# Hybrid encoder layer in fp32: second weight operand ahead only where the first pass runs, the shift sums moved ahead, transposes in two sets of banks, partial sums multiplied where they are added

## The chip, the cores and the metric

The kernel runs on one core of a Trainium2 chip. The metric is the device time of one execution in microseconds (us). TensorE (PE) does the matmuls, VectorE (DVE) and ScalarE (ACT) the elementwise work, GpSimd (POOL) clears a few tiles and issues some transfers, SyncE (SP) issues nearly all transfers (DMAs). Each engine takes its own instructions strictly in the order in which they stand.

## The reference, cut to what matters

```python
mod = silu(c) @ w_ada + b_ada                 # c: one row of 2048
shift, scale, gate = split(mod, 3)
h = rmsnorm(x, pre_g) * (1 + scale) + shift   # x: 1024 rows of 2048
proj = h @ w_in                               # 2048 x 4608
q, k, v, gate_a, u, gate_p = split(proj)
y_a = windowed_gqa(q, k, v, ...) * silu(gate_a)
y_p = multiscale_pool(u, ...) * silu(gate_p)
g_a, g_p = split(sigmoid(h @ w_merge + b_merge))   # 2048 x 4096
merged = g_a * (y_a @ w_br_attn) + g_p * (y_p @ w_br_pool)
out = x + gate * rmsnorm(merged @ w_out, post_g)
```

All of it is in fp32.

## The kernel before

**Matmuls.** Each fp32 operand is split into a high and a low part (`split`: ACT writes `hi`, DVE writes `lo`), and a product is three matmuls (high by high, high by low, low by high). `h @ w_in` and `h @ w_merge` are made with Strassen's seven products (Winograd's form) for two blocks of 128 output columns, a "pair". `strassen` is a generator that makes one pair, a product per step: X from B11, V from T3, Z from T2, X from B21, V from T4, Z from T1, Z from B22 (X, V, Z are banks of PSUM; B11 ... B22 are operands made from `h`; each weight operand is `whi`/`wlo`, made from a loaded `raw` or from a difference `ws`). Each bank is read by ACT or DVE before its next product may start. A product with four row blocks is 12 matmuls of 128x512; in the ramp it has two row blocks and six matmuls.

**Stages.** (1) The start, to about 90 us: `x` is transposed (`XT` banks on PE, taken to `xT` by ACT and DVE), matrix-vector sums (`GEMV`) give the scale and later the shift of the first columns (`PM` turns a sum into columns), and the first four pairs are multiplied without their shift by plain blocks (`PB`); each finished block `c` is copied by ACT and stored to `ramp_d` by POOL's queue (`put_by`). (2) The ramp, to about 212 us: pairs 4 to 7 for the first four row blocks (`js` 0 and 1), then all eight for the rest (`js` 2 and 3). In the second half each stored part is loaded, multiplied by `rb` (`times`, L285) and added to a product (L260). (3) The first pass, to about 723 us: the other pairs, for the first half of the rows of the weights. (4) From about 723 us the second pass adds the other half to the parts in `part_d`; its start also builds four sums of `w_out` (`sw` loaded, summed on DVE, stored to `ws_dS`), and from about 860 us it carries attention. (5) The branches and the output product.

**What sets the order.** The start is an order written by hand: instructions passed through `keep` keep the program's order on their engine. Elsewhere a scheduler orders each engine's instructions from its own costs, so a generator that yields at another place can stand otherwise on DVE, ACT and SP far from the edit. `late` holds a pair back, so that its last product (Z from B22) is made two steps into the next pair. `SEEDED` names two PSUM tags of one bank each; the tags `mm`, `at`, `sc` have two banks.

Of the kernel before, what the change touches and what calls it, by code (L numbers as in the profile page):

```python
# [43 lines left out]
def encoder_layer(ctx: ExitStack, tc: tile.TileContext, x, c, table, w_ada, b_ada, pre_g,  # L44
# [167 lines left out]
    def strassen(w, n0, rows, js, op, ev, finish, part=None, raws=None, given=(), bias=None, factor=None):  # L212
# [70 lines left out]
        def times(*blks):  # L283
            for blk in blks if bias else ():
                nc.vector.tensor_tensor(parts[blk], parts[blk], factor[:, int(blk[1]) - 1], ALU.mult)  # L285
# [4 lines left out]
        first, second = next(wts), next(wts)  # L290
        product(first, "B11", bx, True)
        nc.scalar.activation(bz, bx, AF.Copy)
# [23 lines left out]
        product(prep(a12), "B22", bz)  # L316
        result("12", bz)
# [120 lines left out]
    def norm_row(si):  # L438
        square_of(si, 2, False)
        square_of(si, 3, True)  # L440
        square_of(si, 1, si % 2 == 0, xts[si, 2 + (si % 2 == 0)])
# [218 lines left out]
    def raw_operands(j, s, turned=False):  # L660

        for kh, name in enumerate(("B11", "B21") if s == 0 else ("B12", "B22")):
# [3 lines left out]
            keep(nc.scalar.activation(hi, src, AF.Copy, scale=a))  # L666
            keep(nc.vector.scalar_tensor_tensor(lo, src, a, f32(hi), op0=ALU.mult, op1=ALU.subtract))
# [60 lines left out]
    def ramp_gen(js, i, parts, last, **kw):  # L728
        w, n0 = weight_of(RAMP_ORDER[i])
        dst = block(part_d, RAMP_ORDER[i]) if last else block(ramp_d[i], 0)  # L730
        return strassen(w, n0, rows_in_turn(0), js, op, ev, to_dram(dst), parts, raws.pop(0), **kw)
# [6 lines left out]
    def fetch_wide(half, j):  # L738

        wide[half, j] = wp.tile([P, 2, 512], F32, tag="raw", name=uid("wide"), bufs=4)  # L740
        n0 = COL_K + half * 512
        keep(load(wide[half, j], w_in[2 * j * P:(2 * j + 2) * P, n0:n0 + 512].rearrange("(k p) n -> p k n", p=P)))
# [8 lines left out]
    fetch_wide(0, 0)  # L751
    for si in range(4, 8):
        fetch_row(si, (0,))
    claim_turned(range(4))
# [85 lines left out]
    def turn_next():  # L840
        s, ks = rounds.popleft()
        turn_part(s, ks, SEEDED)
        for k in ks:
            take_turned(s, k, False)
# [22 lines left out]
    for k in range(2):  # L867
        take_turned(0, k, k == 1)
# [1061 lines left out]
```

## Time and profile before

| | us |
|---|---|
| median of 3 runs | 2108.41 (2107.81 to 2109.29) |
| the profiled execution, its own time | 2110.96 |
| its span (first to last instruction) | 2109.2 |
| PE busy | 2076.3 |
| DVE busy | 1552.8 |
| ACT busy | 1113.3 |
| POOL busy | 47.3 |
| mean granted TensorE clock | 0.997 |

The time is that of one core from end to end; 1.8 us of the profiled execution's time lie outside its span. Busy times of the engines overlap. In rows of the timeline, the first number is the start in us, the second the duration, and the bracket says how long the engine stood idle before it and what ended that. Rows with "x4" join four instructions.

### The profile page before, as it was taken

To read this page: it belongs to the slowest core of one execution; us is meant where nothing else is said; L and a number is where in the kernel's file an instruction comes from. 1 tells how busy PE (TensorE), PEld (TensorE's weight loads), DVE (VectorE), ACT (ScalarE), POOL (GpSimd) and SP (SyncE) were. 2 spreads that over 40 slices of the span, in tenths; PEclk is the share of its full clock that TensorE was granted. 3 is DMA by queue.
4 is the path that set the end of the run, shared out by engine and by line. 5 is a ranking of instruction groups with operands and counts; after the bars stand their busy time and mean duration, and the time that the engine had idled before them with its cause. 6 is when DMAs were issued, how large, how long until landed. Compare 5 with 4: busy or idle time off the path is not lost.

```text
span 2109.2 us, 29056 instructions
## 1 busy us (share of the span) xinstructions
PE 2076.3 (98%) x9526; PEld 1703.7 (81%) x9526; DVE 1552.8 (74%) x2799; ACT 1113.3 (53%) x2126; POOL 47.3 (2%) x150
## 2 busy tenths in 40 slices
PE   8999999999999999999999999999999999999998
PEld 5677888788888887788888888888888788888886
DVE  4689677777566775777777678857957977889667
ACT  5664444444564633665666544333745644767654
POOL 1100000001000000000000000010000000000000
PEclk9999999999999999999999999999999999999999
DMA  9877777887575467654545476765745566686897
GB/s 357 305 255 253 262 262 223 281 289 246 186 242 191 136 224 239 232 166 161 194 160 162 153 243 223 223 236 174 254 153 170 176 199 194 221 313 203 298 332 246
DMA packets 302608, 476.61 MB, mean 226 GB/s; under 512 B 24306, under 2 KB 139098, under 8 KB 302456
## 3 DMA queue, kind: packets, MB, share of 16 engines
q1 hardware_dynamic: 296192, 457.79, 66.1%
q0 software_dynamic: 5200, 14.85, 1.8%
q10 hardware_dynamic: 1064, 2.11, 0.3%
q8 instruction: 75, 1.23, 0.3%
q14 instruction: 77, 0.63, 0.1%
HBM read 346.70 MB, written 130.05 MB: 226 GB/s over the span
## 4 chain that ended last, share of the span: by engine, by line
PE 86%; DVE 5%; DMA 5%; issue 2%; ACT 1%; POOL 0%; SPq 0%; DVEq 0%; POOLq 0%; ACTq 0%
PE Z L237 28%; PE X L237 19%; PE V L237 18%; PE Z L1637 2%; PE Z L1638 2%; PE Z L1639 2%; PE V L1638 1%; PE V L1637 1%; PE V L1639 1%; PE X L1639 1%; PE X L1638 1%; PE X L1637 1%; DVE wlo L97 1%; PE PT L1347 1%; DMA bias_d<-line_d 1%
## 5 line engine op out<-in xcount | busy, mean ns | idle before, releaser
L96 ACT ACTIVATE whi<-raw 128x512 fp32r<-128x512 f32 (+1 forms) x528 | 314.7, 600 | 487.6 <-PE Z L237 238.0
L97 DVE TENSOR_TENSOR wlo<-raw,whi 128x512 fp32r<-128x512 f32 (+1 forms) x528 | 339.4, 649 | 149.8 <-PE Z L237 112.9
L97 DVE TENSOR_TENSOR wlo<-wr,whi 128x512 fp32r<-128x512 f32 x224 | 150.6, 689 | 51.3 <-ACT whi L96 47.3
L96 ACT ACTIVATE whi<-wr 128x512 fp32r<-128x512 f32 x224 | 138.5, 629 | 86.2 <-DVE wlo L97 31.7
L103 DVE TENSOR_TENSOR raw<-raw,raw 128x512 f32<-128x512 f32 x76 | 52.4, 690 | 98.7 <-DMA raw<-in_w_merge_dram 60.8
L96 ACT ACTIVATE whi<-ws 128x512 fp32r<-128x512 f32 (+1 forms) x88 | 53.0, 603 | 77.1 <-PE X L237 62.2
L237 PE MATMUL X<-B11h,whi 128*128 128x512 f32 x328 | 90.5, 394 | 2.4 <-DVE part L103 2.4
L237 PE MATMUL Z<-T2h,whi 128*128 128x512 f32 x328 | 89.2, 391 | 3.2 <-ACT whi L96 3.0
L237 PE MATMUL Z<-T2h,wlo 128*128 128x512 f32 x328 | 89.5, 392 | 2.2 <-DVE wlo L97 2.2
L237 PE MATMUL Z<-T1l,whi 128*128 128x512 f32 x328 | 89.4, 390 | 1.1 <-DVE T1l L97 1.1
L237 PE MATMUL V<-T3h,whi 128*128 128x512 f32 x328 | 89.5, 392 | 0.8 <-DVE u L103 0.8
L237 PE MATMUL X<-B11l,whi 128*128 128x512 f32 x328 | 90.1, 393 | 0.0
L237 PE MATMUL X<-B21h,whi 128*128 128x512 f32 x328 | 90.0, 393 | 0.0
L237 PE MATMUL Z<-B22h,whi 128*128 128x512 f32 x328 | 89.9, 392 | 0.0
L237 PE MATMUL Z<-T1h,whi 128*128 128x512 f32 x328 | 89.7, 390 | 0.0
L237 PE MATMUL V<-T4h,whi 128*128 128x512 f32 x328 | 89.5, 391 | 0.0
L237 PE MATMUL X<-B21l,whi 128*128 128x512 f32 x328 | 89.3, 391 | 0.0
L237 PE MATMUL X<-B21h,wlo 128*128 128x512 f32 x328 | 89.1, 391 | 0.0
L237 PE MATMUL X<-B11h,wlo 128*128 128x512 f32 x328 | 88.9, 390 | 0.0
L237 PE MATMUL Z<-B22l,whi 128*128 128x512 f32 x328 | 88.9, 390 | 0.0
L237 PE MATMUL V<-T3l,whi 128*128 128x512 f32 x328 | 88.9, 390 | 0.0
L237 PE MATMUL V<-T4h,wlo 128*128 128x512 f32 x328 | 88.9, 390 | 0.0
(419 smaller groups left out, 4913.0 us busy)
## 6 DMA issues: line engine op xcount, KB each, us to landing
part<-part_d SPq DMA_DIRECT2D x136, 256.0 KB, 4.7
ada<-in_w_ada_dram SPq DMA_DIRECT2D x128, 256.0 KB, 5.7
raw<-in_w_merge_dram SPq DMA_DIRECT2D x64, 512.0 KB, 5.0
wr<-ws_dS SPq DMA_DIRECT2D x60, 512.0 KB, 5.3
raw<-in_w_in_dram SPq DMA_DIRECT2D x56, 512.0 KB, 4.4
wr<-in_w_out_dram SPq DMA_DIRECT2D x48, 512.0 KB, 5.1
proj_d<-part SPq DMA_DIRECT2D x68, 256.0 KB, 2.2
sw<-in_w_out_dram SPq DMA_DIRECT2D x64, 256.0 KB, 5.2
```

The source lines that it names most:

```text
L96: ins = (nc.scalar.activation(hi, src, AF.Copy), nc.vector.tensor_tensor(lo, src, f32(hi), ALU.subtract))
L97: nc.vector.tensor_tensor(lo, src, f32(hi), ALU.subtract))
L103: return (eng or nc.vector).tensor_tensor(o, a, b, ALU.add)
L237: nc.tensor.matmul(ps, w_[:, i], op[mov][j][m_], start=fresh and i == 0 and n == 0, stop=i == nj - 1 and n == 2, skip_group_check=True)
L1347: nc.tensor.transpose(pt[:, i * P:(i + 1) * P], p[:, i * P:(i + 1) * P], ident)
L1637: nc.tensor.matmul(pb, hi, w[0], start=first, stop=False, skip_group_check=True)
L1638: nc.tensor.matmul(pb, lo, w[0], start=False, stop=False, skip_group_check=True)
L1639: nc.tensor.matmul(pb, hi, w[1], start=False, stop=last, skip_group_check=True)
```

## The change

In words:

- `strassen` has a new argument `ahead`. With it (ramp and first pass) the second weight operand (`ws`) is still made before the first product; without it (all later pairs of `strassen`) it is made after the first step.
- `times` takes one part and is called just before or after the product to which the part is added: "22" after the V product is issued, "21" after Z from T2, "11" after X from B21, "12" after Z from B22. Before, the multiplications stood one to three steps earlier.
- At the start, `fetch_wide` loads the first wide weights in two halves; the sum for the scale columns (`g[4]`) is taken ahead of the first transposes; `xT` is taken from the `XT` banks right after the raw operands; two squares move from ACT to DVE.
- The shift `GEMV` and its scaled rows (`scale_row`) stand ahead of block (2,"22"), its `PM` right behind that block. The four rounds of transposes of tiles 4 to 7 use `SEEDED` and `at` banks in turn, and the takes stand behind the shifted operands (`put_shifted`) they were ahead of; the third weight operand (`first_given(2)`) moves up.
- The pool of evictions in the ramp's second half has 7 buffers instead of 6; the raw weights of the second pair of the first pass are loaded at step 0 instead of 2.

```diff
-        def times(*blks):
-            for blk in blks if bias else ():
+        def times(blk):
+            if bias:
                 nc.vector.tensor_tensor(parts[blk], parts[blk], factor[:, int(blk[1]) - 1], ALU.mult)
...
-        first, second = next(wts), next(wts)
+        first = next(wts)
+        second = next(wts) if ahead else None
         product(first, "B11", bx, True)
         nc.scalar.activation(bz, bx, AF.Copy)
+        yield
+        product(second or next(wts), "T3", bv, True)
         times("22")
-        yield
-        product(second, "T3", bv, True)
         p7 = read("p7", "22", bv)
-        times("21")
         yield
         product(next(wts), "T2", bz)
+        times("21")
         u2 = read("u2", "21", bz)
-        times("11", "12")
         yield
         product(prep(a12), "B21", bx)
+        times("11")
         result("11", bx)
...
         product(prep(a12), "B22", bz)
+        times("12")
         result("12", bz)
...
-    fetch_wide(0, 0)
+    fetch_wide(0, 0, 0, 256)
     for si in range(4, 8):
         fetch_row(si, (0,))
+    fetch_wide(0, 0, 256, 512)
...
+    g[4]()
     turn_part(0, (0, 1), SEEDED)
-    g[4]()
     turn_part(0, (2, 3), ("mm", "mm"))
-    wide_weights(0, 0)()
-    raw_operands(0, 0, True)
-    for k in (2, 3):
-        take_turned(0, k, k == 3)
+    raw_operands(0, 0, True, lambda: wide_weights(0, 0)())
+    for k in (0, 2, 1, 3):
+        take_turned(0, k, k % 2 == 1)
...
     raw_operands(0, 1, True)
-    for k in range(2):
-        take_turned(0, k, k == 1)
     turn_part(1, (2, 3), SEEDED)
...
     put_by(3, "21")
-    turn_next()
-    sums_over()
-    whole_block(2, "22")
-    put_by(2, "22")
     for si in range(4, 8):
         scale_row(si)
     g = row_sums(scz, shift_tile, shift_columns)
     for step in g[:4]:
         step()
+    sums_over()
+    whole_block(2, "22")
+    put_by(2, "22")
+    g[4]()
     first_given(0)
     first_given(1)
-    turn_next()
-    g[4]()
-    whole_block(3, "12")
+    takes = turn_next(SEEDED)
     put_shifted("B11", lambda j: block_of(j, 0, 0), shift(0))
-    put_by(3, "12")
-    turn_next()
+    for take in takes:
+        take()
...
     put_shifted("T3", lambda j: block_of(j, 0, 1), lambda j: dif[:, j:j + 1])
+    whole_block(3, "12")
+    put_by(3, "12")
+    takes = turn_next(("at", "at"))
+    for take in takes:
+        take()
+    put_shifted("T2", t2.__getitem__, shift(1))
     whole_block(3, "22")
     put_by(3, "22")
-    turn_next()
-    put_shifted("T2", t2.__getitem__, shift(1))
+    first_given(2)
+    takes = turn_next(SEEDED) + turn_next(("at", "at"))
     put_shifted("B21", lambda j: block_of(j, 1, 0), shift(1))
-    first_given(2)
+    for take in takes:
+        take()
     fill_last()
...
-    pev = ramp.enter_context(pool("rampev", 6))
+    pev = ramp.enter_context(pool("rampev", 7))
```

The matmuls of the products stay in their order outside the first 340 or so of PE's rows, but for one exchange of two neighbouring groups. What moves on the other engines shows at four places.

ACT, the first block of the start, before. `whi<-wide` is the high part of the first weights, B11h ... B22h the first operands, `XT_461`, `XT_478` and so on the banks that hold transposed `x`:

```order
L515 ACTIVATE acc_456<-GEMV_439 128x256
L787 ACTIVATE whi_488<-wide_166 128x512
L666 ACTIVATE B11h_190<-XT_461,modc 128x512
L666 ACTIVATE B21h_194<-XT_462,modc 128x512
L482 ACTIVATE xT_184<-XT_478 128x512
L666 ACTIVATE B12h_202<-XT_512,modc 128x512
L666 ACTIVATE B22h_198<-XT_513,modc 128x512
L482 ACTIVATE xT_176<-XT_461 128x512
```

The same place after:

```order
L518 ACTIVATE acc_457<-GEMV_440 128x256
L669 ACTIVATE B11h_191<-XT_469,modc 128x512
L795 ACTIVATE whi_490<-wide_166 128x512
L669 ACTIVATE B21h_195<-XT_470,modc 128x512
L485 ACTIVATE xT_177<-XT_469 128x512
L485 ACTIVATE xT_185<-XT_479 128x512
L669 ACTIVATE B12h_203<-XT_515,modc 128x512
L669 ACTIVATE B22h_199<-XT_516,modc 128x512
```

The copy that empties the first `SEEDED` bank (`xT<-XT_461`, now `XT_469`) moved ahead of the operands of the second half of the rows; on DVE the copy of the other `SEEDED` bank moved likewise.

ACT ahead of the third product of the ramp's first pair, before. `Z<-X` copies the first product's bank, which the third product (Z from T2) adds to:

```order
L810 ACTIVATE c_1015<-PB_1002 128x512
L482 ACTIVATE xT_350<-XT_1018 128x512
L482 ACTIVATE xT_1_353<-XT_1019 128x512
L712 ACTIVATE T2h_358<-tf_850,modc 128x512
L712 ACTIVATE T2h_366<-tf_852,modc 128x512
L712 ACTIVATE B21h_194<-xT_180,modc 128x512
L712 ACTIVATE B21h_210<-xT_0_188,modc 128x512
L292 ACTIVATE Z_1054<-X_1053 128x512
L251 ACTIVATE p_240_1069<-V_1055 128x512
L96 ACTIVATE whi_1040<-raw_370 128x256
```

After:

```order
L818 ACTIVATE c_1008<-PB_995 128x512
L96 ACTIVATE whi_1013<-raw_371 128x256
L717 ACTIVATE B21h_195<-xT_181,modc 128x512
L717 ACTIVATE B21h_211<-xT_0_189,modc 128x512
L485 ACTIVATE xT_343<-XT_1017 128x512
L485 ACTIVATE xT_347<-XT_1018 128x512
L485 ACTIVATE xT_351<-XT_1027 128x512
L485 ACTIVATE xT_1_354<-XT_1028 128x512
L717 ACTIVATE B22h_199<-xT_183,modc 128x512
L717 ACTIVATE B22h_215<-xT_1_190,modc 128x512
L293 ACTIVATE Z_1055<-X_1054 128x512
```

The third weights (`whi<-raw`) moved ahead of the copy Z<-X, and so did two more takes of `xT` and both B22h.

DVE in the ramp's second half, at the pair whose parts are numbered 2091 to 2097, before. `part<-part,rb` is `times`, `wlo<-raw` the low part of the third product's weights:

```order
L285 TENSOR_TENSOR part_2095<-part_2095,rb 128x512
L285 TENSOR_TENSOR part_2097<-part_2097,rb 128x512
L260 SCALAR_TENSOR_TENSOR p_519_2165<-V_2140,bias_1775,part_2091 128x512
L97 TENSOR_TENSOR wlo_2183<-raw_1831,whi_2182 128x256
L97 TENSOR_TENSOR wlo_2206<-raw_1831,whi_2205 128x256
```

After (the parts are numbered 2090 to 2096):

```order
L285 TENSOR_TENSOR part_2094<-part_2094,rb 128x512
L106 TENSOR_TENSOR ws_2251<-raw_1953 128x256
L97 TENSOR_TENSOR wlo_2183<-raw_1832,whi_2182 128x256
L260 SCALAR_TENSOR_TENSOR p_519_2165<-V_2140,bias_1776,part_2090 128x512
L97 TENSOR_TENSOR wlo_2205<-raw_1832,whi_2204 128x256
L97 TENSOR_TENSOR wlo_2219<-raw_1832,whi_2218 128x256
```

The multiplication of the fourth part (2097, now 2096) is no longer ahead of that `wlo`; it stands 14 rows further on.

DVE near the start of the second pass, before. `raw<-raw,raw` is the first sum of the next pair's weights and reads both its `raw` tiles; `part<-X` empties the X bank that the next pair's first product fills:

```order
L97 TENSOR_TENSOR wlo_7757<-raw_7609,whi_7756 128x512
L97 TENSOR_TENSOR wlo_7793<-raw_7777,whi_7792 128x512
L103 TENSOR_TENSOR u_1584_7714<-u_1584_7714,part_7615 128x512
L103 TENSOR_TENSOR raw_7777<-raw_7777,raw_7779 128x4x128
L106 TENSOR_TENSOR raw_7777<-raw_7777 128x4x128
L103 TENSOR_TENSOR part_7617<-X_7621,part_7617 128x512
```

After:

```order
L97 TENSOR_TENSOR wlo_7758<-raw_7610,whi_7757 128x512
L103 TENSOR_TENSOR raw_7778<-raw_7778,raw_7780 128x4x128
L97 TENSOR_TENSOR wlo_7794<-raw_7778,whi_7793 128x512
L103 TENSOR_TENSOR u_1584_7715<-u_1584_7715,part_7616 128x512
L106 TENSOR_TENSOR sw_7691<-sw_7689,sw_7691 128x512
L106 TENSOR_TENSOR raw_7778<-raw_7778 128x4x128
L106 TENSOR_TENSOR sw_7693<-sw_7693,sw_7691 128x512
L103 TENSOR_TENSOR part_7618<-X_7622,part_7618 128x512
```

The sum that reads both `raw` tiles moved up two rows, and two sums of `w_out` (`sw`) came between it and `part<-X`. On SP, the load of the second of these `raw` tiles stands at the same place behind four loads of `sw`, but the store `ws_dS4` that the last of them waits for moved up five rows:

```order
L1083 DMA ws_dS_97<-sw_7520 128x512
L335 DMA proj_d<-u_1553_7546 128x512
L209 DMA part_7613<-part_d 128x512
L209 DMA part_7615<-part_d 128x512
L335 DMA proj_d<-p_1544_7496 128x512
L209 DMA part_7617<-part_d 128x512
L209 DMA part_7619<-part_d 128x512
L1083 DMA ws_dS_100<-sw_7526 128x512
L1072 DMA sw_7688<-in_w_out_dram 128x512
```

```order
L1092 DMA ws_dS_97<-sw_7521 128x512
L1092 DMA ws_dS_100<-sw_7527 128x512
L337 DMA proj_d<-part_7455 128x512
L1081 DMA sw_7689<-in_w_out_dram 128x512
L337 DMA proj_d<-u_1553_7547 128x512
L209 DMA part_7614<-part_d 128x512
L209 DMA part_7616<-part_d 128x512
L209 DMA part_7618<-part_d 128x512
```

The first of the two is before, the second after: `ws_dS_100` (the fourth store of a round) now stands right behind the third instead of behind six transfers.

More of the change, by code (lines that the diff above doesn't have):

```diff
@@ L210, in load_parts, with strassen @@
         return parts
-    def strassen(w, n0, rows, js, op, ev, finish, part=None, raws=None, given=(), bias=None, factor=None):
+    def strassen(w, n0, rows, js, op, ev, finish, part=None, raws=None, given=(), bias=None, factor=None, ahead=False):
         nj = len(js)
@@ L666, in raw_operands @@
             keep(nc.scalar.activation(hi, src, AF.Copy, scale=a))
+            if kh == 0:
+                between()
             keep(nc.vector.scalar_tensor_tensor(lo, src, a, f32(hi), op0=ALU.mult, op1=ALU.subtract))
@@ L730, in ramp_gen @@
         dst = block(part_d, RAMP_ORDER[i]) if last else block(ramp_d[i], 0)
-        return strassen(w, n0, rows_in_turn(0), js, op, ev, to_dram(dst), parts, raws.pop(0), **kw)
+        return strassen(w, n0, rows_in_turn(0), js, op, ev, to_dram(dst), parts, raws.pop(0), ahead=True, **kw)
     def ramp_raws(i, js):
@@ L736, in encoder_layer, with fetch_wide @@
     raws, wide = [], {}
-    def fetch_wide(half, j):
-        wide[half, j] = wp.tile([P, 2, 512], F32, tag="raw", name=uid("wide"), bufs=4)
+    def fetch_wide(half, j, n1=0, n2=512):
+        if n1 == 0:
+            wide[half, j] = wp.tile([P, 2, 512], F32, tag="raw", name=uid("wide"), bufs=4)
         n0 = COL_K + half * 512
-        keep(load(wide[half, j], w_in[2 * j * P:(2 * j + 2) * P, n0:n0 + 512].rearrange("(k p) n -> p k n", p=P)))
+        keep(load(wide[half, j][:, :, n1:n2],
+                  w_in[2 * j * P:(2 * j + 2) * P, n0 + n1:n0 + n2].rearrange("(k p) n -> p k n", p=P)))
     pc = bank(SEEDED[1], "pc")
```

16 lines of the change are left out of this document (8 added, 8 removed).

## The prediction

> **What bounds the kernel.** I read the busy times first, then a table of stretches (length; busy time and count of PE, its weight loads, DVE, ACT, POOL; granted clock; DMA share; GB/s), then TensorE's timeline wherever it stood still.
>
> ```profile
> PE 2076.3 (98%) x9526; PEld 1703.7 (81%) x9526; DVE 1552.8 (74%) x2799; ACT 1113.3 (53%) x2126; POOL 47.3 (2%) x150
> 0.00:30.00 30.00, 20.02 (x128) 11.09 (x129) 10.55 (x25) 10.91 (x24) 4.91 (x37) 1.00 0.97 329
> 30.00:90.00 60.00, 56.04 (x269) 42.77 (x268) 41.87 (x95) 46.73 (x97) 12.07 (x41) 0.97 1.06 378
> 90.00:213.00 123.00, 120.64 (x569) 91.09 (x568) 104.24 (x226) 68.43 (x145) 0.74 (x3) 1.00 0.71 237
> 213.00:723.00 510.00, 508.96 (x2278) 418.38 (x2277) 351.01 (x529) 240.48 (x443) 6.75 (x13) 1.00 0.72 234
> 723.00:870.00 147.00, 140.82 (x609) 114.44 (x608) 100.57 (x163) 62.64 (x107) 0.00 (x0) 0.99 0.72 238
> 870.00:2109.00 1239.00, 1229.81 (x5683) 1025.93 (x5681) 944.58 (x1768) 684.09 (x1312) 22.87 (x56) 1.00 0.64 211
> ```
>
> PE is the bound: its matmuls are not changed, so time can come only from its idle time, span less busy: 9.98 us in the first 30, 3.96 to 90, 2.36 to 213, 1.04 in the first pass, 6.18 in the first 147 us of the second, 9.19 after. The change moves instructions in all of these but the fourth and the last. Their idle time, one by one (the bracket is the idle time and its releaser):
>
> ```profile
> 22.18 0.33 PE L474 MATMUL XT<-ident,xt 128*128 128x128 f32 x1 [1.80 <-ACT xT L482]
> 23.23 0.66 PE L474 MATMUL XT<-ident,xt 128*128 128x128 f32 x4 [0.71 <-DVE xT L480]
> 71.42 0.66 PE L495 MATMUL PM<-ident,acc 128*128 128x128 f32 x4 [1.68 <-ACT acc L515]
> 85.04 0.73 PE L237 MATMUL Z<-T2h,whi 128*128 128x512 f32 x2 [2.29 <-ACT whi L96]
> 188.64 0.73 PE L237 MATMUL Z<-T2h,wlo 128*128 128x512 f32 x2 [1.61 <-DVE wlo L97]
> 208.01 0.72 PE L237 MATMUL Z<-T2h,whi 128*128 128x512 f32 x2 [0.75 <-ACT whi L96]
> 738.83 0.50 PE L237 MATMUL Z<-T1l,whi 128*128 128x512 f32 x1 [0.42 <-DVE T1l L97]
> 740.03 0.50 PE L237 MATMUL Z<-T1l,whi 128*128 128x512 f32 x1 [0.70 <-DVE T1l L97]
> 819.62 1.87 PE L237 MATMUL X<-B11h,whi 128*128 128x512 f32 x4 [1.88 <-DVE part L103]
> 841.11 1.20 PE L237 MATMUL X<-B11h,whi 128*128 128x512 f32 x4 [0.57 <-DVE part L103]
> 868.18 0.38 PE L1324 MATMUL SCORE<-k,qhi 128*128 128x256 f32 x1 [2.27 <-ACT k L96]
> ```
>
> Matmul ends are modelled; from start to start each stall is some 0.15 us longer. Two of them are followed by a stretch at half clock (third figure from the end: the granted clock):
>
> ```profile
> 86.02:89.43 3.41, 3.41 (x9) 2.63 (x9) 2.80 (x7) 2.43 (x7) 0.58 (x2) 0.50 1.11 343
> 819.88:823.29 3.41, 3.41 (x9) 2.67 (x9) 3.41 (x7) 1.56 (x4) 0.00 (x0) 0.50 0.55 206
> ```
>
> Half of 3.41 us is 1.7 us of lost work each. The stall at 819.62 thus costs 1.9 + 1.7.
>
> **The start.** These rows carry the first block and the third product:
>
> ```profile
> 14.83 0.63 ACT L787 ACTIVATE whi<-wide 128x512 fp32r<-128x512 f32 x1 [3.51 <-DMA wide<-in_w_in_dram]
> 20.38 0.69 ACT L666 ACTIVATE B12h<-XT,modc 128x512 fp32r<-128x512 f32 x1 [3.28 <-PE XT L474]
> 23.97 0.47 PE L804 MATMUL PB<-B12h,whi 128*128 128x512 f32 x1
> 68.34 2.55 ACT L466 ACTIVATE xt<-xt,rstd 128x512 f32<-128x512 f32 x4
> 79.26 1.09 ACT L482 ACTIVATE xT<-XT 128x512 f32<-128x512 f32 x2 [0.17 <-PE XT L474]
> 82.13 0.62 PE L237 MATMUL V<-T3h,wlo 128*128 128x512 f32 x2
> 81.46 1.33 ACT L712 ACTIVATE B21h<-xT,modc 128x512 fp32r<-128x512 f32 x2
> 82.69 0.58 ACT L292 ACTIVATE Z<-X 128x512 f32<-128x512 f32 x1
> 66.19 0.37 POOL L425 MEMSET xT<- 128x1 f32 x4 [3.19 <-PE GEMV L511]
> ```
>
> First block: the transposes at 22.18 and 23.23 wait for copies that stood behind B12h and B22h. Now these copies stand ahead, where ACT was idle for 3.28 us. So both stalls go (2.5 us of idle), and B11h and a half as wide `whi` begin without the whole `wide` tile. I replayed the ACT and DVE queues with the rows' durations: the block that starts at 23.97 starts at 20.7, and the work behind it 3.0 us earlier. That carries through the plain blocks as long as `x` and the shift weights land in time; no PE row from there to 65 us names a DMA as its releaser, so I let it carry in full.
>
> Shift and third product: PM waits 1.68 us at 71.42 because the copy of the sum stands behind four scalings (2.55 us). With the sums ahead of block (2,"22"), 12 matmuls cover it. POOL's clearing waits for the sums too (3.19 us), and three stores by POOL now stand behind it, at about 62 us, where the sums end in the replay; nothing reads them before the ramp's second half. PE would then be through the second product at 76.8 instead of 82.75. But ACT is not: Z<-X (at 82.69), which the third product needs, is now behind four `xT` copies, both B21h and both B22h. At 0.5 us a copy and 0.62 a shifted operand (as these rows start behind one another), I get its end at 80.7, against 85.04: 4.3 us for the whole start, 1.3 of them here. Bounds: 8 us (the copy waits for nobody, PE follows the product directly) and 3.0 (what the first block gives; the old stall stays). I take 4.3, the replay's. The stall is then about 4 us, less two matmuls of 0.25; so the half clock behind it stays, at no difference.
>
> **The ramp's second half.**
>
> ```profile
> 186.90 0.69 DVE L285 TENSOR_TENSOR part<-part,rb 128x512 f32<-128x512 f32 x1 [2.47 <-DMA part<-ramp_d]
> 188.17 0.75 DVE L97 TENSOR_TENSOR wlo<-raw,whi 128x256 fp32r<-128x256 f32 x2
> 205.77 0.68 DVE L285 TENSOR_TENSOR part<-part,rb 128x512 f32<-128x512 f32 x1
> 207.04 0.41 DVE L106 TENSOR_TENSOR raw<-raw 128x256 f32<-128x256 f32 x1
> ```
>
> DVE stands 2.47 us in `times` for a part that has not landed, and the `wlo` that PE waits for at 188.64 stands behind it. In the new order that `times` is 14 rows behind the `wlo`, and a seventh buffer lets the load go earlier. At 208.01 PE waits for the third weights, whose sum (207.04) stands behind a `times` (205.77) and a read of V, 0.6 us each; the read now comes after it, so the sum comes 0.66 earlier. The two stalls, start to start, are 1.77 and 0.91; of these 1.77 + 0.66 = 2.4 us go. DVE is busy for 104.24 of the stage's 123 us, so multiplications that are pushed back can delay a later `result`, which frees a bank; I take 2.2, between 0 and 2.7.
>
> **The start of the second pass.**
>
> ```profile
> 733.28 0.69 DVE L103 TENSOR_TENSOR p<-V,part 128x512 f32<-128x512 f32 x1 [2.42 <-DMA part<-part_d]
> 738.10 0.68 DVE L97 TENSOR_TENSOR T1l<-h,T1h 128x512 fp32r<-128x512 f32 x1
> 817.55 0.69 DVE L103 TENSOR_TENSOR raw<-raw,raw 128x512 f32<-128x512 f32 x1 [6.55 <-DMA raw<-in_w_in_dram]
> 818.88 0.68 DVE L103 TENSOR_TENSOR part<-X,part 128x512 f32<-128x512 f32 x1
> 806.04 0.45 SPq L1083 DMA_DIRECT2D ws_dS<-sw  x1
> 806.53 4.78 SPq L1072 DMA_DIRECT2D sw<-in_w_out_dram  x4
> 811.35 0.45 SPq L187 DMA_DIRECT2D raw<-in_w_in_dram  x1
> ```
>
> At 733.28 DVE has waited for a part; four T1l follow among other rows, 0.6 us each, and the last two are late. The new order does the last T4l before that wait and puts fewer rows among the T1l: the last ends at about 738.2, PE needs it at 738.5. Both stalls go, 1.56 us start to start; I take 1.4 (0 to 1.56).
>
> At 817.55 DVE has stood 6.55 us for the next pair's second `raw` tile, and `part<-X` (to 819.57), which frees the X bank, is two rows behind. That `raw` is issued at 811.35, since SP stands in four `sw` loads; the last of them waits for the store issued at 806.04. The store now stands behind its predecessor, at about 799, and SP does not stand there: I get the `raw` issued at 807.1 and, at the same 6.2 us, landed at 813.3. But the waiting sum has moved up: `part<-X` is the sixth row behind it and starts at 813.4 + 6 x 0.6 = 817.0 and ends at 817.7; PE wants the bank at 817.6. So 0.1 or 0.2 us of the 1.9 stays, too little idle for the half clock: 3.4 us. Bounds: 3.6 (all goes) and -2.4 (the tile lands as late as before, and four more rows of 0.6 us lie ahead of `part<-X`). I take 2.7, near the replay but not at it, since the store's new time is the least sure of its steps. At 841.11 the same cause costs 0.73 start to start; the tile comes earlier by the same shift: 0.6.
>
> The two squares moved to DVE (0.6 us each) lie where DVE has gaps (41.87 busy of 60); the split load is one issue more on SP. Nothing for either; were the gaps gone, 1.2 us.
>
> [...] Rows: a PE idle of 2.29 us and one of 1.88 led to half clock, one of 2.27 (at 868.18) did not. [...]
>
> **Sum.** 4.3 + 2.2 + 1.4 + 2.7 + 0.6 = 11.2 us off the profiled execution's 2110.96: 2099.8. That execution is 2.55 us above the median of 2108.41, so 2097.2 beside the runs shown; I say 2097.5.
>
> **Rivals.**
> 1. Another stall meets the clock. Half-speed stretches start on one grid of 3.41 us (from 86.02 to 819.88 are 215 lengths), and the stall at 868.18 missed because it lay across a boundary. In the changed kernel all of it comes about 11 us earlier relative to the grid, and a stall of 2.3 can fall inside one length, in about (3.4 - 2.3)/3.4, a third of positions. Price 1.7: 2099.2. Chance 0.16.
> 2. The start gives its gain back: ACT's chain or late `x` brings the third product to 85 again. Then only the other 6.8 stay: 2101.6. For it: that stretch moves 378 GB/s at a DMA share of 1.06, so nothing can land earlier; against: in the trace PE waits there for ACT, not for transfers. 0.12.
> 3. The change does not do what it says: the late parts and the late `raw` are only met by another row. Then the first block's 3.0 is all: 2105.4, within what a measurement can tell from no change (0.2%, 4.2 us). For it: both waits end on a DMA. 0.12.
> 4. Slower: the sum of the two `raw` tiles, moved up, stops DVE in each pair from 784 to 861 ahead of `wlo` and `part<-X`. If the tiles land as late as at 817.55, each of the five pairs pays up to 2.4 + 1.7 = 4.1 us, 20 us, and with 8 gained elsewhere the time is 2121. It costs once a tile lands later than about 813.3 (817.6 less seven rows), and decides when three pairs are hit. Against: the stores that hold the loads come earlier. 0.06.
>
> My forecast without these has 0.54. The range takes in the ends of the terms: 2092 (8 at the start, all other stalls gone) and, with rival 3, 2106. Faster by over 0.2%: 0.54 + 0.16 + 0.12 = 0.82, less 0.02 for the forecast's weak end; within: 0.14; slower: 0.06. The forecast's own range is 2093 to 2100.
>
> **What would show it.** The GEMV behind the first block near 24 us instead of 26.9; Z<-T2h near 80.7, released by ACT's Z<-X, with half clock behind; no `times` waiting ahead of a `wlo` near 180; no idle time at T1l; X<-B11h near 810 with under 1 us of idle and full clock. It is wrong if ACT's chain at 76 to 81 waits for DVE's `raw` sums, if the second `raw` still lands after 817 less what was gained before, or if a new half-speed stretch appears.

## The result and the profile after

| | before, us | after, us |
|---|---|---|
| median of the first measurement | 2108.34 | 2095.76 (2094.22 to 2098.2) |
| the profiled execution, its own time | 2110.96 | 2096.28 |
| its span | 2109.2 | 2094.5 |

The ratio is 0.9941, with a 95% interval of 0.9924 to 0.9958: faster by 12.6 us, where 10.9 were forecast. Measured twice more, beside other runs of the kernel before, the change gave 0.9944 (0.9928 to 0.996) and 0.9949 (0.9936 to 0.9963), some 10 us each by the medians. The first figure is at the good end; 10 to 12 us is the fair reading.

The table of stretches of the changed kernel, in the columns of the prediction's:

```profile
0.00:30.00 30.00, 23.63 (x142) 13.83 (x143) 13.18 (x31) 13.76 (x29) 4.89 (x37) 1.00 0.97 331
30.00:90.00 60.00, 56.24 (x271) 41.87 (x270) 43.07 (x98) 43.37 (x91) 11.96 (x41) 0.97 1.07 378
90.00:213.00 123.00, 123.00 (x580) 94.74 (x579) 107.70 (x230) 70.06 (x147) 0.74 (x3) 1.00 0.75 253
...
723.00:870.00 147.00, 146.42 (x654) 121.08 (x653) 105.33 (x178) 69.38 (x121) 0.00 (x0) 1.00 0.74 247
```

PE's idle time in the first 30 us falls from 9.98 to 6.37, in the ramp from 2.36 to none, in the first 147 us of the second pass from 6.18 to 0.58. Between 30 and 90 us it is hardly less (3.76 for 3.96), which the start's missing microsecond will come from. Now TensorE's timeline at the places that the prediction named (the bracket is idle time and releaser):

```profile
23.62 1.93 PE L514 MATMUL GEMV<-ada,scz 128*32 128x256 f32 x32
52.01 1.98 PE L465 MATMUL RB<-diag,ones 128*128 128x512 f32 x4 [0.96 <-DVE diag L459]
81.94 1.22 PE L237 MATMUL Z<-T2h,whi 128*128 128x512 f32 x2 [2.18 <-ACT Z L293]
86.23 0.61 PE L237 MATMUL V<-T4h,whi 128*128 128x512 f32 x2
183.62 0.62 PE L237 MATMUL Z<-T2h,wlo 128*128 128x512 f32 x2
731.01 1.07 PE L237 MATMUL Z<-T1l,whi 128*128 128x512 f32 x4
808.98 1.07 PE L237 MATMUL X<-B11h,whi 128*128 128x512 f32 x4
852.90 0.38 PE L1333 MATMUL SCORE<-k,qhi 128*128 128x256 f32 x1 [0.24 <-ACT k L96]
```

The rows at 183.62, 731.01 and 808.98 have no bracket: there, in the ramp, at T1l and at X<-B11h, PE does not wait any more. Z<-T2h still waits for ACT's copy, as forecast, but at 81.94 instead of 80.7, and a wait at RB (52.01), which the profile before does not have, is new. Half clock follows the wait at Z<-T2h, as forecast (the length behind it, third figure from the end):

```profile
81.61:85.02 3.41, 3.08 (x7) 2.48 (x8) 2.10 (x6) 2.23 (x7) 1.11 (x2) 0.50 1.10 348
```

On ACT the copy (81.28) comes behind both B21h, four `xT` and both B22h, and none of these waits:

```profile
76.92 1.32 ACT L717 ACTIVATE B21h<-xT,modc 128x512 fp32r<-128x512 f32 x2
78.14 2.03 ACT L485 ACTIVATE xT<-XT 128x512 f32<-128x512 f32 x4
80.05 1.34 ACT L717 ACTIVATE B22h<-xT,modc 128x512 fp32r<-128x512 f32 x2
81.28 0.61 ACT L293 ACTIVATE Z<-X 128x512 f32<-128x512 f32 x1
```

DVE in the second half of the ramp and at the sum of the `raw` tiles:

```profile
181.34 0.42 DVE L97 TENSOR_TENSOR wlo<-raw,whi 128x256 fp32r<-128x256 f32 x1
803.29 0.69 DVE L103 TENSOR_TENSOR raw<-raw,raw 128x512 f32<-128x512 f32 x1 [3.70 <-DMA raw<-in_w_in_dram]
806.91 0.68 DVE L103 TENSOR_TENSOR part<-X,part 128x512 f32<-128x512 f32 x1
```

The `wlo` of the ramp does not wait. The sum of the `raw` tiles still does, 3.70 instead of 6.55 us, but `part<-X` behind it ends at 807.59, before PE wants the bank at 808.98. SP's queue shows why:

```profile
785.61 3.62 SPq L1092 DMA_DIRECT2D ws_dS<-sw  x4
...
794.36 1.54 SPq L1081 DMA_DIRECT2D sw<-in_w_out_dram  x3
795.94 4.06 SPq L187 DMA_DIRECT2D raw<-in_w_in_dram  x2
```

```profile
799.62 0.38 SPq L187 DMA_DIRECT2D raw<-in_w_in_dram  x1
```

The four stores stand together, and SP does not stand in the `sw` loads ahead of `raw` (1.54 us for three, where four took 4.78). The row of two `raw` loads joins two issues. The first, at 795.94, is the tile that the sum at 803.29 waits for. The second, at 799.62 (the row by itself), is for the pair after that and lands when the sum has begun.

How far ahead of the profile before PE is, place by place, as the difference of the same matmul's starts:

| where | before | after | ahead | gained on the way | forecast |
|---|---|---|---|---|---|
| Z<-T2h, first pair | 85.04 | 81.94 | 3.1 | 3.1 | 4.3 |
| Z<-T2h, `wlo` | 188.64 | 183.62 | 5.0 | 1.9 | |
| Z<-T2h, `whi` | 208.01 | 201.75 | 6.3 | 1.2 | 2.2 for the ramp |
| Z<-T1h, `wlo`, behind T1l | 740.37 | 731.91 | 8.5 | 2.2 | 1.4 |
| X<-B11h | 819.62 | 808.98 | 10.6 | 2.2 | 2.7 with the next row |
| V<-T3h, behind the half clock | 824.06 | 811.70 | 12.4 | 1.7 | |
| X<-B11h, next pair | 841.11 | 828.02 | 13.1 | 0.7 | 0.6 |
| first SCORE | 868.18 | 852.90 | 15.3 | 2.2 | 0 |

The ramp ends between the third and the fourth row: X<-B11h, with which the first pass starts, is at 213.60 before and at 207.19 after, 6.4 us ahead. So 3.3 of the 6.4 come from the ramp in all, another 0.4 from a smaller wait early in the first pass (V<-T3h at 273.19 before, at 266.41 after), and 1.7 from T1l. Behind the first SCORE 0.6 is lost again.

### The profile page after: what moved, and what is told of

It reads as the page before. It is cut to its first block, busy times and chain, and to the rows that moved or that the text cites. A ratio compares the mean times of both kernels' runs of the same rounds, so it can differ in the third digit from the quotient of the medians.

```text
span 2094.5 us, 29063 instructions
## 1 busy us (share of the span) xinstructions
PE 2073.1 (99%) x9526; PEld 1703.2 (81%) x9526; DVE 1555.2 (74%) x2803; ACT 1113.4 (53%) x2122; POOL 47.1 (2%) x150
## 3 DMA queue, kind: packets, MB, share of 16 engines
q10 hardware_dynamic: 1064, 2.11, 0.3%
## 4 chain that ended last, share of the span: by engine, by line
PE 92%; DMA 4%; DVE 2%; ACT 1%; issue 0%; SPq 0%; DVEq 0%; ACTq 0%
PE Z L237 31%; PE V L237 20%; PE X L237 20%; PE Z L1646 2%; PE Z L1648 2%; PE Z L1647 2%; DMA ada<-in_w_ada_dram 2%; PE V L1648 1%; PE V L1646 1%; PE X L1648 1%; PE X L1646 1%; PE V L1647 1%; PE X L1647 1%; PE PT L1356 1%; PE PB L812 1%; DMA xt<-in_x_dram 1%
## 5 line engine op out<-in xcount | busy, mean ns | idle before, releaser
L237 PE MATMUL Z<-T2l,whi 128*128 128x512 f32 x328 | 89.1, 391 | 0.0
L237 PE MATMUL V<-T4l,whi 128*128 128x512 f32 x328 | 88.8, 390 | 0.0
```

Source lines behind the costliest of these rows:

```text
L237: nc.tensor.matmul(ps, w_[:, i], op[mov][j][m_], start=fresh and i == 0 and n == 0, stop=i == nj - 1 and n == 2, skip_group_check=True)
```

## The experiments

Each kernel ran beside the kernel before, on the same chip.

| kernel | median, us | ratio to before (95%) |
|---|---|---|
| start_only | 2105.93 | 0.998 (0.9969 to 0.9992) |
| ramp_only | 2104.23 | 0.9981 (0.9972 to 0.9991) |
| ahead_only | 2100.86 | 0.9965 (0.9951 to 0.9978) |
| copy_first | 2095.63 | 0.9936 (0.9922 to 0.995) |
| after_again | 2097.84 | 0.9944 (0.9928 to 0.996) |
| after_pool6 | 2100.64 | 0.996 (0.9945 to 0.9975) |
| sums_by_pool | 2117.59 | 1.004 (1.0027 to 1.0052) |
| four_stores_less | 2095.49 | 0.9934 (0.9919 to 0.9948) |
| copy_first_again | 2093.01 | 0.9929 (0.9917 to 0.9941) |
| after_third | 2097.87 | 0.9949 (0.9936 to 0.9963) |
| after_ahead_all | 2102.34 | 0.9972 (0.9963 to 0.9981) |
| copy_first_k | 2094.07 | 0.9934 (0.9921 to 0.9947) |

### One part at a time

**start_only**: the kernel before with the edits of the start alone.

```diff
-    turn_next()
-    sums_over()
-    whole_block(2, "22")
...
+    sums_over()
+    whole_block(2, "22")
+    put_by(2, "22")
+    g[4]()
...
+    raw_operands(0, 0, True, lambda: wide_weights(0, 0)())
```

> The kernel before with the edits of the start alone (copies, shift sums, transposes in two sets of banks, split load, two squares on DVE). Theory (the stalls are independent, each edit brings its own stalls): Z<-T2h of the ramp's first pair near 81.9 us instead of 85.0, released by ACT's Z<-X, and the stalls at 188.6, 208, 739, 819 and 868 as before, each about 3 us earlier; 2108.3 - 3.2 = 2105.1 us. Rival (what the start wins is lost again in the ramp, which waits for transfers): the ramp's stall at 188 grows and the time is 2107 to 2108. Rival (an earlier start moves the loads of the ramp as well, so the stalls at 188 and 208 shrink without their own edit): 2102.

Measured: 0.2% faster. The third product of its profile:

```profile
82.11 1.22 PE L237 MATMUL Z<-T2h,whi 128*128 128x512 f32 x2 [2.18 <-ACT Z L292]
184.12 0.73 PE L237 MATMUL Z<-T2h,wlo 128*128 128x512 f32 x2 [0.18 <-DVE wlo L97]
```

The start is worth about 3 us, not 4.3, and it takes most of the ramp's first stall along (0.18 us of idle for 1.61), a gain that it shares with the ramp's edits. So the last rival came in part: the stall at 188.6 shrank without its own edit, the one at 208 stayed (0.7 us). The stalls of the second pass stay, 1.50 and 2.11 us at the two X<-B11h.

**ramp_only**: the multiplications moved, seven buffers, the fetch at step 0.

```diff
-        times("22")
         yield
         product(second, "T3", bv, True)
+        times("22")
...
-    pev = ramp.enter_context(pool("rampev", 6))
+    pev = ramp.enter_context(pool("rampev", 7))
```

> The kernel before with the edits of the ramp alone (multiplications at the product to which the part is added, seven buffers, one load of the first pass earlier). Theory: the stalls of 1.77 and 0.91 us at 188.6 and 208.0 and the small ones behind them go, 3.5 us, everything else stays; 2104.8 us. Rival (the multiplications were only half of it, the order of the start is needed too): the two stalls stay in part, 2106 to 2107.

Measured: 0.19% faster. The ramp's row in the table of stretches:

```profile
90.00:213.00 123.00, 123.00 (x583) 93.84 (x582) 107.05 (x232) 69.22 (x146) 0.74 (x3) 1.00 0.74 249
```

PE has no idle time there, and at the start of the first pass it is 3.3 us ahead (X<-B11h, 213.60 before). In the second pass it meets the old stalls again, one with half clock behind it (granted 0.50 from 839.43 to 842.84 us).

**ahead_only**: the second weights later in the second pass alone.

```diff
-        first, second = next(wts), next(wts)
+        first = next(wts)
+        second = next(wts) if ahead else None
...
-        product(second, "T3", bv, True)
+        product(second or next(wts), "T3", bv, True)
```

> The kernel before with the second weights made one step later in the second pass, nothing else. Theory: the T1l stalls at 739 go (1.7), the stall of 2.0 at 819.6 with its half clock (1.7), the one of 0.7 at 841 and, because the sums of w_out and the loads behind them come earlier on DVE and SP, the SCORE stall at 868 too (2.2): together 8.3 us, 2100.0. Rival (the stall at 868 went because the whole attention start meets other transfers in the changed kernel, not by this edit): SCORE still waits about 2 us, 2102.2.

Measured: 0.35% faster, 7.6 us by the medians. T1l and X<-B11h no longer wait:

```profile
813.48 1.07 PE L237 MATMUL X<-B11h,whi 128*128 128x512 f32 x4
84.63 0.73 PE L237 MATMUL Z<-T2h,whi 128*128 128x512 f32 x2 [2.29 <-ACT whi L96]
```

The second row is a surprise: the start is that of the kernel before, with the same stall of 2.29 us, and yet no half clock follows; it is taken up in the last section. The expectation held for T1l and X<-B11h, not for the first SCORE: PE still waits 1.63 us there (at 858.79), as the rival said. Of the three parts this is the largest. Their sum is 0.74%, the whole 0.51 to 0.59%: within the intervals, and part of the difference is known, since start and ramp both take the stall at 188.64 away.

### Is the store the cause of the late `raw` tile?

**sums_by_pool**: the kernel before, with the stores that SP's loads wait for given to POOL's queue.

```diff
-                store(ws_rows(name)[:, j, i * 512:(i + 1) * 512], t)
+                nc.gpsimd.dma_start(ws_rows(name)[:, j, i * 512:(i + 1) * 512], t)
```

> The kernel before, with the stores of the four sums of w_out issued by POOL instead of SP and nothing else. Theory (the load of the second raw tile is late because SP stands for a store that it issues late itself): the store leaves as soon as its sum is made, the raw tile lands some 3 us earlier, the stall at 819.6 falls from 2.0 us to under 0.5 with no half clock, the one at 841 goes; the T1l stalls at 739 stay; 2108.4 - 4 = 2104.4. Rival (DVE's order, its sums among the weights, holds the bank): 819.6 stays over 1.5 us, 2108.

Measured: 0.4% slower. But at the place in question, in PE's and DVE's timelines:

```profile
825.62 1.20 PE L237 MATMUL X<-B11h,whi 128*128 128x512 f32 x4
822.47 0.69 DVE L103 TENSOR_TENSOR raw<-raw,raw 128x512 f32<-128x512 f32 x1 [3.45 <-DMA raw<-in_w_in_dram]
601.20 1.11 PE L1208 MATMUL b<-ident,xt 128*128 128x128 f32 x4 [4.87 <-ACT xt L1219]
```

The stall of 1.88 us is gone, and DVE waits 3.45 us for the tile instead of 6.55, with `strassen` as it was. The `raw` load is issued at 816.57, which is 2.8 us earlier than before when the time is counted by PE's matmuls. That fits the late store as the cause, but this run alone doesn't prove it, since the scheduler made another order for the whole; after_ahead_all below has the late store back, and the wait with it. The stall at the next X<-B11h, which should have gone, stayed (0.74 us for 0.57). The time says nothing on the question: in the new order SP issues a row of `x` at 592.45 behind `sw` loads, ACT waits 6.29 us for it (at 598.11), and PE 4.87 us at 601.20, with half clock behind.

### The whole with one part undone

**after_ahead_all**: the changed kernel with the second weights ahead everywhere.

```diff
-    def strassen(..., ahead=False):
+    def strassen(..., ahead=True):
```

> The changed kernel with the second weights ahead in the second pass too, that is without that one part of the change. Theory (the parts add): the T1l stalls (1.6), the one at about 810 (2.0, with or without a half clock of 1.7) and the one at about 831 (0.7 to 2.3) are back, start and ramp as in the changed kernel: 2096.5 + 5.5 = 2102. Rival (earlier start and ramp have moved the second pass's transfers, so that these stalls no longer need the edit): 2097 to 2098.

Measured: 2102.34 beside 2097.87 of the changed kernel, 4.5 us more. The stalls of the second pass are back:

```profile
731.39 0.50 PE L237 MATMUL Z<-T1l,whi 128*128 128x512 f32 x1 [0.41 <-DVE T1l L97]
810.93 1.19 PE L237 MATMUL X<-B11h,whi 128*128 128x512 f32 x4 [1.79 <-DVE part L103]
812.44:815.85 3.41, 3.41 (x10) 2.67 (x9) 3.41 (x7) 1.63 (x3) 0.00 (x0) 0.50 0.78 287
```

```profile
808.85 0.69 DVE L103 TENSOR_TENSOR raw<-raw,raw 128x512 f32<-128x512 f32 x1 [6.46 <-DMA raw<-in_w_in_dram]
797.90 5.30 SPq L1081 DMA_DIRECT2D sw<-in_w_out_dram  x4
```

X<-B11h waits 1.79 us, for 1.88 before, with half clock behind it, and the next X<-B11h 0.52 for 0.57. Of the two stalls at T1l (0.42 and 0.70 us) one is back. The cause is back as well: a store of the sums is issued just ahead of the four `sw` loads, at 797.41, SP stands 5.30 us in these, `raw` is issued at 803.25, and DVE waits 6.46 us for it. Not all of the 4.5 us is of the second pass's products: the first SCORE waits 2.26 us in this profile, where three of the changed kernel have 0.24 to 1.70.

**after_pool6**: the changed kernel with six buffers of evictions.

```diff
-    pev = ramp.enter_context(pool("rampev", 7))
+    pev = ramp.enter_context(pool("rampev", 6))
```

> The changed kernel with 6 buffers instead of 7 in the ramp's second half. Theory (the place of the multiplications removes the two stalls, the seventh buffer only brings the loads forward): the ramp's second half stays without idle time over 0.3 us, same time, 2095.8. Rival (the buffer is what brings the parts in time): idle times of 1 to 2 us come back between 140 and 205 us, 2097 to 2099.

Measured: 2100.64 beside 2097.84. PE and DVE in the ramp:

```profile
189.72 0.73 PE L237 MATMUL X<-B11h,whi 128*128 128x512 f32 x2 [1.05 <-DVE part L260]
187.71 0.69 DVE L285 TENSOR_TENSOR part<-part,rb 128x512 f32<-128x512 f32 x1 [2.58 <-DMA part<-ramp_d]
```

The place of the multiplications doesn't do it without the buffer: with six buffers the load of the part is as late as before (2.58 us for 2.47), and the wait is met by the row that frees the X bank. The stall moves from Z's `wlo` to X. My third rival described this; the seventh buffer is what keeps it away. In start_only, with six buffers and the multiplications at their old places, the two stalls are no larger (0.18 and 0.7 us), so these profiles show no gain of the new places without the buffer. Whether seven buffers alone would do, no run shows.

### Where the start's 1.2 us went

**four_stores_less**: the changed kernel without four of the 16 stores of `c` by POOL, three of which fall among the issues of `x`'s loads. The second half of the ramp then reads pair 2's parts for pairs 0 and 1, so its output is another.

```diff
-        nc.gpsimd.dma_start(block(ramp_d[i], 0)(blk), t)
+        if (i, blk) not in ((0, "22"), (1, "11"), (1, "21"), (1, "12")):
+            nc.gpsimd.dma_start(block(ramp_d[i], 0)(blk), t)
...
-        parts[i] = load_parts(ev, block(ramp_d[i], 0))
+        parts[i] = load_parts(ev, block(ramp_d[2 if i < 2 else i], 0))
```

> The changed kernel without the stores of four finished blocks of pairs 0 and 1 (1 MB; the second half of the ramp loads pair 2's blocks in their place, so the result is another). Theory (the start is now bound by transfers: POOL's stores come 3 us earlier, among the last rows of x, and hold them up): x's last row lands about 2.6 us earlier (4 x 0.66), the 1.0 us of idle at RB (52 us) goes, the shift sums do not wait either, Z<-T2h comes at about 80.0 instead of 81.9; 2095.8 - 2 = 2093.8. Rival (the wait at RB is DVE's own queue, its two squares more): RB still waits 1 us and the time is the same.

RB's `diag` needs the squares of all `x` rows. Measured, DVE's last square in the kernel before, in the changed one and without the four stores, then PE without them (in the kernel before ACT squares the last rows, until 50.79, and RB at 54.16 does not wait):

```profile
46.98 0.69 DVE L433 SCALAR_TENSOR_TENSOR xt<-xt 128x512 f32<-128x512 f32 x1
```

```profile
49.49 0.69 DVE L435 SCALAR_TENSOR_TENSOR xt<-xt 128x512 f32<-128x512 f32 x1 [0.46 <-DMA xt<-in_x_dram]
```

```profile
47.81 0.69 DVE L435 SCALAR_TENSOR_TENSOR xt<-xt 128x512 f32<-128x512 f32 x1 [1.29 <-DMA xt<-in_x_dram]
50.82 1.88 PE L465 MATMUL RB<-diag,ones 128*128 128x512 f32 x4
80.66 0.73 PE L237 MATMUL Z<-T2h,whi 128*128 128x512 f32 x2 [2.18 <-ACT Z L293]
```

Without the stores RB does not wait, and Z<-T2h starts at 80.66, where the replay had put it. The last row of `x` lands at 47.28 before, at 49.40 after, and at 47.72 without the stores: 1.7 us earlier, where 2.6 were expected. In the five profiles that have this start and all stores (three of the changed kernel, after_ahead_all, after_pool6) RB waits 0.96 to 1.78 us and Z<-T2h starts at 81.94 to 82.64. DVE's two squares more, the rival, are in the order without the stores too, so they are not what RB waits for. PE's 3 us of lead bring POOL's stores 3 us earlier, too, into the stretch in which the last loads of `x` run and the DMA share is 1.07:

```profile
36.52 1.12 POOL L811 DMA_DIRECT2D ramp_d<-c  x2 [30.95 <-ACT c L810]
```

```profile
33.23 1.12 POOL L819 DMA_DIRECT2D ramp_d<-c  x2 [27.67 <-ACT c L818]
```

The first row is before, the second after. The time of the whole is not clearly better (2095.49 beside 2097.84): PE idles 2.5 us at the first SCORE in this profile.

### A copy that stands too late

**copy_first**: the changed kernel with Z<-X ahead of the last two copies of `xT` and of B22h, which move into the ramp's first pair.

```diff
+    for take in turn_next(SEEDED):
+        take()
+    takes = turn_next(("at", "at"))
     first_given(2)
-    takes = turn_next(SEEDED) + turn_next(("at", "at"))
...
-    for take in takes:
-        take()
-    fill_last()
...
+            at.append((0, lambda: [take() for take in takes]))
+            at.append((4, fill_last))
```

> The changed kernel with ACT's copy Z<-X ahead of the last two copies of xT and of both B22h in the ramp's first pair (B22h is made some steps later, the first two copies of xT of the last round stand ahead of the third weights). Theory (that copy's place on ACT sets the third product): Z<-T2h near 79 instead of 81.9, under 1 us of idle, no half clock behind it, V<-T4h near 81.7 instead of 86.2; 2095.8 - 4.5 = 2091.3 us. Rival (the third weights, made of DVE's sums behind T2l, or T2l itself are ready no earlier): no change, 2095.8. Rival (B22h, pushed later, stops PE at Z<-B22h or delays weights): between, 2093 to 2096.

> The kernel with ACT's copy Z<-X ahead, once more, beside the changed kernel. Theory (its 4.6 us up to the first pass are kept, what was lost later in its first profile was the varying wait at SCORE, 1.9 against 0.2 us): V<-T4h again near 81.7 us with no half-speed stretch behind the third product, median 2.5 to 4.5 us under the changed kernel's measured beside it. Rival (a gain at the start is taken back by the waits for transfers at SCORE): within 1 us of it.

Measured: 2095.63 in the first run and 2093.01 in the second, there beside 2097.87 of the changed kernel. PE and ACT in the second:

```profile
78.52 0.73 PE L237 MATMUL Z<-T2h,whi 128*128 128x512 f32 x2
81.81 0.62 PE L237 MATMUL V<-T4h,whi 128*128 128x512 f32 x2
849.90 0.39 PE L1334 MATMUL SCORE<-k,qhi 128*128 128x256 f32 x1 [1.84 <-ACT k L96]
77.89 0.57 ACT L293 ACTIVATE Z<-X 128x512 f32<-128x512 f32 x1
```

The third product no longer waits and the half clock behind it is gone: V<-T4h starts at 81.81 for 86.23, 4.4 us earlier. Some of it is lost at the first SCORE, by a wait of 1.84 us with half clock behind it. This version is faster than both kernels: ratio 0.9929 to before, where the changed kernel beside it had 0.9949, and the three runs of the one (2091.59 to 2095.16) all lie under those of the other (2095.88 to 2098.75). The first run did not stand beside the changed kernel.

**copy_first_k**: the same, with the first keys fetched a side step earlier.

```diff
-                if u % 16 == 0 and e == 0:
+                if u and u % 16 == 0 and e == 0:
...
+        side.append(lambda: take_k(0))
```

> The kernel with the copy Z<-X ahead, and the first keys fetched and split one side step ahead of the first scores instead of in the same step; all later attention steps come one side slot later. Theory (SCORE waits because the keys' load needs the buffers that the queries' split frees, and then lands late): the idle time at the first SCORE falls under 0.5 us, 1 to 2 us faster than the kernel with the copy alone. Rival (the shift of all attention steps by a slot makes other waits): SCORE waits less, the time is the same or up to 3 us longer.

Measured: 2094.07 beside 2093.01 of copy_first, no difference. The first SCORE does not wait in its profile, which speaks for the keys' late load as what PE waited for there; but the 1 to 2 us expected from it are not there, since PE now waits elsewhere: 0.67 and 0.77 us at X<-B11h, and, the longest behind SCORE, 0.94 us for DVE's part of the values (PV at 874.47).

### The changed kernel again

**after_again** and **after_third** are the changed kernel itself, to see how far its stalls belong to one execution.

> The changed kernel once more, unedited, beside the others. Theory (half-speed windows have no fixed place in the program, and the wait at SCORE changes from execution to execution): median 2095 to 2097, its executions spread over some 4 us, and in the profile the half-speed stretch and the idle time at SCORE (0.2 us in the first profile) can stand otherwise, while the stalls at 52, 79 and 82 us are the same to 0.1 us. Rival (both are set by the order): the same stretch at 81.6 to 85.0 and 0.2 us at SCORE again.

> The changed kernel a third time, unedited, as the reference for the three others: 2095 to 2098, idle at SCORE anywhere from 0.2 to 2.6 us.

The first SCORE of after_again, and then PE's and DVE's rows of after_third:

```profile
853.41 0.38 PE L1333 MATMUL SCORE<-k,qhi 128*128 128x256 f32 x1 [0.89 <-ACT k L96]
```

```profile
810.13 1.19 PE L237 MATMUL X<-B11h,whi 128*128 128x512 f32 x4 [1.25 <-DVE part L103]
855.64 0.38 PE L1333 MATMUL SCORE<-k,qhi 128*128 128x256 f32 x1 [1.70 <-ACT k L96]
805.77 0.69 DVE L103 TENSOR_TENSOR raw<-raw,raw 128x512 f32<-128x512 f32 x1 [5.70 <-DMA raw<-in_w_in_dram]
```

The last row is DVE's: in this execution the sum of the `raw` tiles starts 2.5 us later than in the first, and a stall of 1.25 us is back, without half clock. Idle at the first SCORE is 0.24, 0.89 and 1.70 us in three profiles of one kernel. The stalls of the start are not the same to 0.1 us, as after_again expected: at 52 us RB waits 1.78 us in it for 0.96; the waits at 79 and 82 us are the same. The three profiled executions took 2096.28, 2097.24 and 2097.87 us. That the first measurement's median is some 2 us under the later ones for these reasons is not shown.

## Why the prediction was right

The time is within 2 us of the forecast, and the signs of all terms held, by the mechanisms named. The sizes did not all hold, and that the sum came so near is in part luck. By the table of leads the profile gained 14.7 us (3.1 + 3.3 + 0.4 + 1.7 + 3.9 + 0.7 + 2.2 - 0.6), where 11.2 were forecast: the start was put 1.2 too high, the ramp 1.1 and X<-B11h 1.2 too low, and the 2.2 at SCORE were not in the sum at all.

- **Start, 4.3 forecast, 3.1 found** (2.4 and 2.8 in the two later profiles of the changed kernel). The GEMV is at 23.62 (forecast: near 24), and Z<-T2h waits for ACT's Z<-X with half clock behind. The step that failed is "no PE row from there to 65 us names a DMA as its releaser, so I let it carry in full". A row that waits for no transfer says only that the transfers were in time for PE as it stood; with 3 us of lead they were not. four_stores_less shows what held them up. The profile had said so in the share of 1.06 at 378 GB/s, and I used that for a rival and not for the sum. My second rival, late `x`, thus came in part: 1.2 of the 4.3 us. (Its other terms sum to 6.9, not 6.8.)
- **Ramp, 2.2 forecast, 3.3 found.** Both stalls went whole, by 2.7 start to start, and the stage held about 0.6 us more of small waits. The seventh buffer, a half sentence in the prediction, is needed for it.
- **T1l, 1.4 forecast, 1.7 found**, a little over the upper bound of 1.56.
- **X<-B11h, 2.7 forecast, 3.9 found** in the first profile: 2.2 by the stall and 1.7 by the clock. (The bound of 3.6 counted the stall by its idle time, not start to start.) Ahead of this stall PE leads by 8.5 us, so 8.5 is added to put a time of after into the old count. The second `raw` was issued at 795.94, or 804.4 (replay: 807.1), and its sum started at 803.29, or 811.8 (replay: 813.4). The step that failed is "at the same 6.2 us": from issue to sum it took 7.3 us, and 7.1 and 8.1 in the two later profiles. But the issue came 2.7 us earlier than in the replay, and the two errors set each other off, which is luck. In after_third, with 8.1, the sum started at 805.77, and 1.25 us of the stall was back. The mechanism held; the term is what this one transfer makes of it, 2.4 to 3.9. The 1.7 in it hang on the length of the wait, too: at this place one of 1.79 us in after_ahead_all was followed by half clock, one of 1.50 in start_only was not (last section).
- **X<-B11h of the next pair, 0.6 forecast, 0.7 found.**
- **First SCORE, 0 forecast, 2.2 found** in the first profile. It is not by the change as a whole: the wait is 2.27 us before and 0.24, 0.89 and 1.70 in three profiles of the changed kernel, and ramp_only, with the second pass as before, has 0.31.
- **Rival 1** (another stall meets the clock): no new half-speed stretch in the first profile. Its argument was wrong, though: it took the clock's grid as fixed to the program (last section), and its share of positions, a third, is too small. Of the lengths found there that were followed by half clock, the busiest had PE busy for 1.62 us, so idle for 1.79. A stall of 2.3 us holds 0.5 more, so it would be followed by half clock in about (3.41 - 2.3 + 2 x 0.5) / 3.41 of the positions, three fifths (an estimate from these numbers).
- **Rival 4** (DVE stopped in each pair): did not come. Where the sum waited longest in these profiles of the changed kernel, 5.70 us, PE lost 1.25 us once, and not in every pair.

## What to carry to other kernels

A stall is paid by the place that a row has in another engine's queue: one copy moved on ACT gave 4.4 us at its place, where all the edits of the start had given 3.1. When a wait on a transfer is moved away from one row, look which row meets it next, and give the transfer an earlier start too (a buffer more, a store sooner), or the stall only changes its name (in after_pool6 from Z's `wlo`, 1.61 us before, to X, 1.05 us). Where the transfers are as dense as in this start (a DMA share of 1.07), an engine that comes earlier can bring its own stores earlier, into the loads that it needs next (here two of them from 36.52 to 33.23 us).

## What the hardware showed that I had not expected

The half-speed stretches lie on a grid of 3.41 us within one execution. Where a profile has two or more of them, they start a whole number of lengths of 3.413 us apart: 215 in the profile before (from 86.02 to 819.88), 221 in start_only (from 81.75 to 836.09), 239 in ramp_only (from 23.64 to 839.43), 214 and 14 in after_ahead_all (from 81.99 to 812.44 and 860.23), 3, 169 and 80 in sums_by_pool (from 14.13 to 24.37, 601.23 and 874.29). But the grid does not start with the program. Counted from the first instruction, its phase was 0.69 us in the profile before, 3.10, 0.39 and 1.41 in three profiles of the changed kernel, and from 0.07 to 3.24 in the other ten. Cut along its own grid, each profile shows how busy PE was in the length ahead of half clock. Lengths of this grid in the kernel before, then one of ahead_only:

```profile
82.61:86.02 3.41, 1.12 (x5) 0.84 (x5) 2.71 (x6) 2.62 (x6) 0.54 (x2) 1.00 1.08 375
...
816.47:819.88 3.41, 1.53 (x7) 0.99 (x6) 2.30 (x4) 0.28 (x1) 0.00 (x0) 1.00 0.52 188
...
864.26:867.67 3.41, 1.65 (x8) 1.03 (x6) 2.18 (x4) 1.88 (x5) 0.00 (x0) 1.00 0.96 297
867.67:871.08 3.41, 2.55 (x12) 2.04 (x13) 2.90 (x6) 3.36 (x6) 0.00 (x0) 1.00 1.01 311
```

```profile
82.99:86.40 3.41, 1.77 (x7) 1.28 (x8) 2.71 (x6) 2.62 (x7) 1.12 (x2) 1.00 1.08 367
```

A length in which PE was busy for 1.12 or 1.53 us was followed by half clock, one with 1.65 or 1.77 was not. In all 14 profiles, between 17 us and the last 15 us, 18 lengths had PE busy for 0.03 to 1.62 us, and all 18 were followed by half clock; those with 1.65 us or more were not. So the same stall of 2.29 us costs 1.4 us more (from Z<-T2h to V<-T4h 4.45 us for 3.03) or nothing, by where the grid happens to lie in that execution. In this stretch the least idle time in a length that was followed by half clock was 1.79 us (3.41 less 1.62), so no stall under that, alone in its length, led to it. Outside of the stretch the bound is not the same: in sums_by_pool a length at 10.72 us with PE busy for 2.13 us was followed by half clock. Why, no run shows.
